# Summing the first heads' queries, keys and values quarter by quarter, in PSUM banks that stay open while the modulation arrives

## The chip, the cores and the metric

One core of one Trainium2 chip runs the whole program. The metric is the device time in microseconds of one execution, the median of several runs; lower is better.

## What is computed

Two transformer blocks and then two mixer layers over 512 latent tokens and 256 context tokens of 1024 features, batch 1. Only the front of the first block matters here:

```
mod_lat = silu(c)    @ ada_w[0] + ada_b[0]       # 6 x 1024: shift, scale, gate, twice
mod_ctx = silu(c_ctx) @ ada_w[0] + ada_b[0]
u_lat = rms_norm(x,   g_mix) * (1 + sc1)  + sh1      # 512 x 1024
u_ctx = rms_norm(ctx, g_mix) * (1 + csc1) + csh1     # 256 x 1024
q, k, v = split(u @ na_wqkv, 3)                      # 16 heads of 64, latent and context
q, k = rms_norm(q, na_q_gain), rms_norm(k, na_k_gain)    # per head
y_lat = neighborhood_attention(q_lat, k_lat, v_lat, k_ctx, v_ctx, rpb) @ na_wo
y_ctx = context_attention(q_ctx, k_ctx, v_ctx) @ na_wo
```

Everything is float32. The kernel writes each matrix operand as a high and a low part (`hi`, `lo`) and sums three products, hi·hi, hi·lo and lo·hi.

## The kernel before

Activations lie feature by feature: `hl` holds the latent tokens as 8 blocks of 128 features by 512 tokens, `hc` the context as 8 blocks by 256. The modulated activations are `uhl`/`ull` (latent, high and low) and `uhc`/`ulc` (context).

**The order of the work.** The kernel is a Python program that issues instructions; a planner orders each engine's instructions before the run, by the program's order and by when it reckons that an instruction's operands are there. It can draw a later instruction ahead of one that isn't ready. At run time each engine takes its own queue strictly in the planned order. Tiles of one name share a fixed number of buffers; a new tile waits until the last reader of the buffer's previous tile is done. `banks(...)` gives names to the eight PSUM banks by turns: `banks(mm="01", ...)` hands out banks 0 and 1 alternately to every projection.

**The start (L595 to L617).** `load_x` issues the activations on SP's DMA queue (3.1 MB). Then a loop over four quarters `b` of the modulation: `ada(0, 0, "AD", b)` loads four pieces of 512 KB of `ada_w` into six borrowed buffers (`vt`, `ky`, `qx`, two each), multiplies them with silu(c) (L183), copies the sums out (L202), turns them into columns (L206) and adds the bias (L216). A quarter gives shift and scale of two feature blocks, and `mod_gain` (L256) the gain. At `b == 1` the token norms `rstd` (L263 to L275) are issued, at `b == 3` the weights of the first head pair's queries and keys (`qk_w(0)`: 4 DMAs of 256 KB, then L128 and L129 split them into `whi`, `wlo`). After the loop stand the modulation of all eight blocks (`modulate`, L278 to L290: product on VectorE, shift on ScalarE, low part on VectorE or GpSimd), the loads of three position biases, `qk_proj(0)` and `v_proj(0)`.

**Projections.** `lin` (L147) sums queries or keys: for each of two column groups j it runs 24 terms (8 feature blocks, three products) into a latent bank (512 columns) and a context bank (256). All high weights come first, the eight low-weight terms last. `tok` (L156) sums the values with the tokens on the partitions: six token tiles of 128, each 24 terms of 256 columns, one PSUM bank each. `v_proj` loads its own weights (2 DMAs of 512 KB). `whi` and `wlo` have two buffers each, the raw weights four.

**Head norms.** `head_norm` (L293 to L308) takes a finished sum from its bank (Square on ScalarE L297, product with the gain on VectorE L298), sums squares over a head by a matmul (L300, into bank 7), and needs three of the six temporaries; `stack_q` and `stack_k` (L327 to L342) then write the high and low parts. One head pair needs four such norms: query latent, query context, key latent, key context.

**The loop behind.** For eight head pairs `hp`, five units `b` each: scores (L347), maximum and exponentials (L314, L650), transposes (L656), attention (L677). At `b == 1` the projections of the next pair are issued (`qk_proj(hp + 1)`, then three tiles of the next values); here `mm` is banks 0 and 1, scores take 3 and 4, transposes 5, attention 6, and low weight parts are made on GpSimd.

Of the kernel before, what the change touches and what calls it, by code (L numbers as in the profile page):

```python
# [19 lines left out]
D = 1024  # L20
# [42 lines left out]
def kernel(ctx: ExitStack, tc: tile.TileContext, A, out, stop_after=None):  # L63
# [83 lines left out]
    def lin(outs, w, ms, k0=0, k1=KD, start=True, stop=True):  # L147

        hi, lo = w
        terms = [(a, i, j) for i in range(k0, k1) for a, j in ((hi, 1), (hi, 2))] + [(lo, i, 1) for i in range(k0, k1)]  # L150
        for n_, (a, i, j) in enumerate(terms):
            for o in outs:
                nc.tensor.matmul(out=o[0], lhsT=a[:, i, ms], rhs=o[j][:, i, :],  # L153
                                 start=(start and n_ == 0), stop=(stop and n_ == len(terms) - 1))

    def tok(ps, wv, xs):  # L156

        hi, lo = wv
        terms = [(x, hi, i) for i in range(KD) for x in xs] + [(xs[0], lo, i) for i in range(KD)]
        for n_, (x, w, i) in enumerate(terms):  # L160
            nc.tensor.matmul(out=ps, lhsT=x[:, i, :], rhs=w[:, i, :], start=(n_ == 0), stop=(n_ == len(terms) - 1))  # L161
# [222 lines left out]
    with tc.tile_pool(name="first", bufs=1) as fp, scratch("scr1", 6, 2):  # L384
# [149 lines left out]
        def neighborhood():  # L534
# [4 lines left out]
            with tc.tile_pool(name="na", bufs=1) as ap_:  # L539
# [4 lines left out]

                def qk_proj(hp, w):
                    qk = []
                    for j in range(2):
                        pl, pc = mm_tile(), mm_tile()[:, :NCTX]
                        lin([(pl, *ul), (pc, *uc)], w, slice(128 * j, 128 * j + 128))
                        g = vec("na_k") if j else nag  # L550
                        if j:
                            y = ky_tile()
                            stack_k(y, LAT, head_norm(pl, NLAT, g))
                            stack_k(y, slice(NLAT, NT), head_norm(pc, NCTX, g))
                            qk.append(y)
                        else:
                            x = qx_tile()
                            lo = next(lows)
                            stack_q((x, lo), LAT, head_norm(pl, NLAT, g))
                            nc.scalar.activation(out=x[:, :, NLAT:QC], in_=x[:, :, 0:64].bitcast(F32), func=AF.Copy)  # L560
                            nc.vector.tensor_copy(out=lo[:, :, NLAT:QC], in_=lo[:, :, 0:64].bitcast(F32))
                            stack_q((x, lo), slice(QC, QC + NCTX), head_norm(pc, NCTX, g))
                            qk.append((x, lo))
                    qks[hp] = qk

                def qk_w(hp, lo_eng=None):
                    return load_w([(0, 128, wqkv[:, 128 * hp:128 * hp + 128]),
                                   (128, 128, wqkv[:, D + 128 * hp:D + 128 * hp + 128])], KD, 256, lo_eng)

                def v_proj(g, ts=range(6)):  # L570
# [898 lines left out]
```

## Time and profile before

| | us |
|---|---|
| median of 3 runs | 2670.5 |
| lowest, highest | 2670.2, 2676.28 |
| the profiled execution, its own time | 2669.24 |
| its span, first to last instruction | 2667.5 |
| TensorE (PE) busy | 2581.6 |
| VectorE (DVE) busy | 1611.9 |
| ScalarE (ACT) busy | 1249.7 |
| GpSimd (POOL) busy | 314.9 |

A row of the timeline gives the start in us, the busy time in us, the engine, the line, the operation, the tile written and the tiles read, the shape and the count; in brackets stands how long the engine idled before it and what ended that. PE's busy time contains modelled ends of pipelined matmuls; from start to start two matmuls can be closer than one lasts. SPq is SP's queue of DMA issues.

### The profile page before, as it was taken

The numbers are of one execution on the slowest core, as the hardware profiler recorded it, in microseconds if no ns is written. First come the engines' busy times: TensorE is split into PE (matmuls) and PEld (weight loads), VectorE is DVE, ScalarE is ACT, GpSimd is POOL, SyncE is SP. The second block draws the span as 40 slices with busy tenths as digits, with TensorE's granted clock in tenths as the row PEclk, the third lists the DMA queues.
The fourth block names the chain that finished last, engine by engine and source line by source line (L and its number), as shares of the span: only waits on it lengthen the run. The fifth ranks groups of instructions, "written<-read, shape, count | busy, mean of one in ns | idle before, by whom it ended". The sixth has DMA issues, their size and how long they took to land.

```text
span 2667.5 us, 40938 instructions
## 1 busy us (share of the span) xinstructions
PE 2581.6 (97%) x15876; PEld 2185.8 (82%) x15876; DVE 1611.9 (60%) x3496; ACT 1249.7 (47%) x2661; POOL 314.9 (12%) x344
## 2 busy tenths in 40 slices
PE   7999999999999999999999999999999999999998
PEld 4877777888888888877788888987778888998887
DVE  5667658676666577688664444755664556523245
ACT  5656556422222223688552323456664554554342
POOL 2221310100000000332010000111101111101011
PEclk9999999999999999999999999999999999999999
DMA  8111324143333342210123333322222232323321
GB/s 258 56 56 53 115 64 156 56 150 113 115 114 118 95 127 64 76 33 17 48 80 98 101 100 95 86 74 67 61 76 79 80 86 80 93 88 95 97 91 54
DMA packets 217634, 237.93 MB, mean 89 GB/s; under 512 B 9824, under 2 KB 179296, under 8 KB 217440
## 3 DMA queue, kind: packets, MB, share of 16 engines
q1 hardware_dynamic: 210464, 229.15, 28.3%
q10 hardware_dynamic: 6976, 6.17, 0.8%
q8 instruction: 125, 2.05, 0.3%
q14 instruction: 69, 0.57, 0.1%
HBM read 233.18 MB, written 2.10 MB: 88 GB/s over the span
## 4 chain that ended last, share of the span: by engine, by line
PE 80%; DVE 10%; ACT 7%; issue 2%; DMA 1%; POOL 0%; DVEq 0%; POOLq 0%; ACTq 0%; SPq 0%
PE mm L153 59%; PE mm L161 7%; PE ST L677 1%; DVE t L281 1%; PE PT L656 1%; PE ST L836 1%; PE PT L819 1%; PE NS L300 1%; DVE acc L269 1%; PE S L347 1%; PE PO L1052 1%; ACT qx L327 1%; DVE wlo L129 1%; ACT whi L128 1%; ACT qx L333 1%
## 5 line engine op out<-in xcount | busy, mean ns | idle before, releaser
L129 DVE TENSOR_TENSOR wlo<-wraw,whi 128x512 fp32r<-128x512 f32 (+1 forms) x580 | 385.7, 704 | 383.6 <-ACT whi L128 248.3
L128 ACT ACTIVATE whi<-wraw 128x512 fp32r<-128x512 f32 (+1 forms) x632 | 353.9, 619 | 475.9 <-PE mm L153 275.1
L153 PE MATMUL mm<-uhl,whi 128*128 128x512 f32 (+1 forms) x1480 | 568.8, 388 | 1.7 <-ACT whi L128 1.6
L153 PE MATMUL mm<-ull,whi 128*128 128x512 f32 (+1 forms) x1480 | 565.6, 385 | 2.9 <-POOL ull L129 2.9
L153 PE MATMUL mm<-uhl,wlo 128*128 128x512 f32 (+1 forms) x1480 | 406.4, 384 | 1.9 <-DVE wlo L129 1.9
L153 PEld LDWEIGHTS mm<-uhl,whi 128*128 128x128 f32 x1480 | 278.0, 188 | 60.4 <-ACT whi L128 4.9
L153 PEld LDWEIGHTS mm<-ull,whi 128*128 128x128 f32 x1480 | 278.2, 188 | 55.2 <-POOL ull L129 4.7
L153 PEld LDWEIGHTS mm<-uhl,wlo 128*128 128x128 f32 x1480 | 268.6, 188 | 55.6 <-DVE wlo L129 2.5
L419 DVE SCALAR_TENSOR_TENSOR hl<-mm,mod,hl 128x512 f32<-128x512 f32 (+1 forms) x156 | 105.3, 680 | 187.5 <-PE mm L153 187.1
L153 PE MATMUL mm<-h1l,whi 128*128 128x512 f32 (+1 forms) x576 | 209.3, 371 | 0.0
L153 PE MATMUL mm<-h1h,whi 128*128 128x512 f32 (+1 forms) x576 | 208.9, 370 | 0.0
L129 POOL TENSOR_TENSOR ull<-t,uhl 128x256 fp32r<-128x256 f32 (+1 forms) x40 | 37.7, 947 | 1091.5 <-ACT uhl L128 997.8
L153 PE MATMUL mm<-h1h,wlo 128*128 128x512 f32 (+1 forms) x576 | 161.8, 369 | 0.0
L161 PE MATMUL mm<-whi,uhl 128*128 128x256 f32 x608 | 152.6, 286 | 0.6 <-DVE t L298 0.5
L161 PE MATMUL mm<-whi,ull 128*128 128x256 f32 x608 | 152.9, 287 | 0.0
L232 DVE SCALAR_TENSOR_TENSOR aacc<-araw,csil,aacc 128x512 f32<-128x512 f32 x196 | 135.2, 746 | 0.0
L475 ACT ACTIVATE t<-mm 128x512 f32<-128x512 f32 (+1 forms) x100 | 47.7, 507 | 171.2 <-PE mm L153 171.2
L153 PE MATMUL mm<-ulc,whi 128*128 128x256 f32 x448 | 124.6, 286 | 1.8 <-POOL ulc L129 1.8
L153 PEld LDWEIGHTS mm<-h1h,whi 128*128 128x128 f32 x576 | 108.6, 189 | 20.1 <-issue 1.0
L153 PE MATMUL mm<-uhc,whi 128*128 128x256 f32 x448 | 124.7, 287 | 0.2 <-ACT uhc L128 0.2
L153 PEld LDWEIGHTS mm<-h1l,whi 128*128 128x128 f32 x576 | 108.6, 189 | 18.7
L161 PEld LDWEIGHTS mm<-whi,uhl 128*128 128x128 f32 x608 | 116.2, 191 | 2.7 <-DVE t L298 1.4
(382 smaller groups left out, 5289.0 us busy)
## 6 DMA issues: line engine op xcount, KB each, us to landing
wraw<-mlp_w SPq DMA_DIRECT2D x128, 512.0 KB, 4.1
wraw<-l_w_in SPq DMA_DIRECT2D x88, 512.0 KB, 4.0
araw<-ada_w SPq DMA_DIRECT2D x112, 256.0 KB, 2.9
wraw<-l_w_out SPq DMA_DIRECT2D x32, 512.0 KB, 3.5
wraw<-ada_w SPq DMA_DIRECT2D x24, 512.0 KB, 4.3
wraw<-l_w_in SPq DMA_DIRECT2D x48, 256.0 KB, 3.4
wraw<-na_wqkv SPq DMA_DIRECT2D x32, 256.0 KB, 4.0
wraw<-swa_wqkv SPq DMA_DIRECT2D x12, 512.0 KB, 3.6
```

Of the source, the lines that this page charges most:

```text
L128: nc.scalar.activation(out=hi, in_=src, func=AF.Copy)
L129: lo_eng.tensor_tensor(out=lo, in0=src, in1=hi.bitcast(F32), op=ALU.subtract)
L153: nc.tensor.matmul(out=o[0], lhsT=a[:, i, ms], rhs=o[j][:, i, :], start=(start and n_ == 0), stop=(stop and n_ == len(terms) - 1))
L161: nc.tensor.matmul(out=ps, lhsT=x[:, i, :], rhs=w[:, i, :], start=(n_ == 0), stop=(n_ == len(terms) - 1))
L232: nc.vector.scalar_tensor_tensor(out=acc[v], in0=raw, scalar=x, in1=acc[v], op0=ALU.mult, op1=ALU.add)
L269: nc.vector.tensor_tensor(out=acc, in0=acc, in1=sq, op=ALU.add)
L281: nc.vector.scalar_tensor_tensor(out=t, in0=h, scalar=gain, in1=r, op0=ALU.mult, op1=ALU.mult)
L300: nc.tensor.matmul(out=st, lhsT=blk, rhs=sq)
L327: nc.scalar.activation(out=x[a, e, c], in_=t[a], func=AF.Copy)
L333: nc.scalar.activation(out=x[b, e, c], in_=t[a], func=AF.Copy)
L419: nc.vector.scalar_tensor_tensor(out=o, in0=ps, scalar=mod[i][:, 8 * which + m, v:v + 1], in1=h, op0=ALU.mult, op1=ALU.add)
L475: nc.scalar.activation(out=a, in_=p, func=AF.Relu)
```

## The change

The four quarters now carry the first projections with them.

- The weights of the first queries and keys are loaded and split right after the activations, ahead of all of `ada_w`; those of the first values right after the first quarter's `ada_w`, their low parts on VectorE.
- Six banks stay open through the loop: banks 0 and 1 for the latent queries and keys, bank 2 for both contexts side by side, banks 3 to 5 for the values, two token tiles in each. A bank that holds two sums is first filled with zeros by a matmul (four in all), as two sums can't both open it.
- After each quarter's `mod_gain` its two feature blocks are modulated, and `lin` and `tok` add the terms of these two blocks (`k0`, `k1`) to the open sums: 12 of the 48 `lin` terms and 36 of the 144 `tok` terms. Only the last quarter closes the banks.
- Behind the loop the head norms stand as before (moved into `qk_heads`); the values leave their banks by three ScalarE copies of 512 columns in place of six of 256.

```diff
-                banks(mm="01234", NS="7", AD="56")
+                w0 = qk_w(0)
+                banks(QL="01", QC="2", V="345", AD="6", NS="7")
+                pq = [bank("QL") for _ in range(2)]
+                pc = bank("QC")
+                pv = [bank("V") for _ in range(3)]
+
+                for x in (pc, *pv):
+                    nc.tensor.matmul(out=x, lhsT=ones, rhs=zero.to_broadcast([128, 512]), start=True, stop=False)
...
                 for b in range(4):
-                    if b == 1:
-                        r = [rstd(h, n) for h, n in ((hlat, NLAT), (hctx, NCTX))]
-                    if b == 3:
-                        w0 = qk_w(0, nc.vector)
                     for _ in ada(0, 0, "AD", b):
                         pass
                     mod_gain(0, "mix", 2 * b, 2 * b + 2)
+                    if b == 0:
+                        r = [rstd(h, n) for h, n in ((hlat, NLAT), (hctx, NCTX))]
+                        wvs[0] = v_w(0)
+                    for k in range(2 * b, 2 * b + 2):
+                        for v, h, u in ((0, hlat, ul), (1, hctx, uc)):
+                            modulate(k, h(k), r[v], gains["gmix0"][:, v, k:k + 1], mod[0][:, k, v:v + 1], u[0][:, k, :], u[1][:, k, :])
+                    for j in range(2):
+                        lin([(pq[j], *ul), (pc[:, 256 * j:256 * j + 256], *uc)], w0, slice(128 * j, 128 * j + 128), 2 * b, 2 * b + 2,
+                            (b == 0, False), (b == 3, b == 3 and j == 1))
+                    for t in range(6):
+                        x, o = (ul, 128 * t) if t < 4 else (uc, 128 * (t - 4))
+                        tok(pv[t // 2][:, 256 * (t % 2):256 * (t % 2) + 256], wvs[0], parts(x, slice(o, o + 128)), 2 * b, 2 * b + 2, False,
+                            b == 3 and t % 2 == 1)
                 scr.pop("ada", None)
-                for k in range(KD):
-                    for v, h, u in ((0, hlat, ul), (1, hctx, uc)):
-                        modulate(k, h(k), r[v], gains["gmix0"][:, v, k:k + 1], mod[0][:, k, v:v + 1], u[0][:, k, :], u[1][:, k, :])
                 for h in range(3):
                     load_bias(h)
-                qk_proj(0, w0)
-                v_proj(0)
+                qks[0] = [qk_heads(j, pq[j], pc[:, 256 * j:256 * j + 256]) for j in range(2)]
+                vts[0] = vt_tile()
+                for x in range(3):
+                    nc.scalar.activation(out=vts[0][:, 2 * x:2 * x + 2, :].rearrange("p t f -> p (t f)"), in_=pv[x], func=AF.Copy)
```

## Rows read from the trace of the kernel before

**Rows 1.** The page, part 1: busy us of each engine, share of the span, instructions

```profile
PE 2581.6 (97%) x15876; PEld 2185.8 (82%) x15876; DVE 1611.9 (60%) x3496; ACT 1249.7 (47%) x2661; POOL 314.9 (12%) x344
```

**Rows 2.** Windows: stretch, length, busy PE, PEld, DVE, ACT, POOL, granted clock, DMA share, GB/s

```profile
0.00:14.79 14.79, 0.00 (x1) 0.00 (x1) 6.67 (x21) 9.12 (x19) 3.79 (x10) 1.00 0.90 292
14.79:20.86 6.07, 6.07 (x28) 2.13 (x29) 2.83 (x7) 2.05 (x4) 0.00 (x0) 1.00 1.09 348
20.86:34.25 13.39, 9.81 (x86) 4.78 (x85) 9.39 (x26) 8.25 (x16) 3.91 (x4) 1.00 1.11 331
34.25:59.68 25.43, 24.79 (x135) 17.23 (x136) 14.96 (x30) 14.01 (x28) 5.06 (x5) 1.00 0.75 229
59.68:81.48 21.80, 19.38 (x152) 18.39 (x150) 14.73 (x23) 14.15 (x32) 9.71 (x8) 1.00 0.17 49
81.48:93.53 12.05, 11.80 (x82) 9.90 (x81) 4.91 (x14) 3.31 (x8) 5.47 (x4) 1.00 0.29 88
93.53:141.06 47.53, 46.11 (x346) 38.72 (x344) 32.13 (x88) 28.68 (x68) 9.74 (x8) 1.00 0.16 45
141.06:189.77 48.71, 45.78 (x344) 38.15 (x343) 33.29 (x88) 30.04 (x71) 14.76 (x12) 1.00 0.24 77
```

**Rows 3.** Waits of PE from 14 to 82 us: total, times, longest

```profile
PE NS L300 <- DVE t L306: 2.4, 2, 2.0
```

**Rows 4.** Timeline: first modulated block, first projection matmul, last quarter's modulation

```profile
24.35 0.72 ACT L289 ACTIVATE uhl<-t,mod 128x512 fp32r<-128x512 f32 x1 [2.46 <-DVE t L281]
...
34.25 0.50 PE L153 MATMUL mm<-uhl,whi 128*128 128x512 f32 x1 [0.24 <-ACT whi L128]
...
46.55 0.24 DVE L216 TENSOR_TENSOR mod<-AD,vecs 128x4 f32<-128x4 f32 x2 [0.81 <-PE AD L206]
```

**Rows 5.** Timeline of SP's queue: the first head pair's weights

```profile
25.36 4.90 SPq L140 DMA_DIRECT2D wraw<-na_wqkv  x4
```

**Rows 6.** Timeline of PE: terms of a later projection, and value terms

```profile
78.60 0.28 PE L161 MATMUL mm<-whi,uhc 128*128 128x256 f32 x1
78.72 0.28 PE L161 MATMUL mm<-whi,ulc 128*128 128x256 f32 x1
...
82.89 0.40 PE L153 MATMUL mm<-ull,whi 128*128 128x512 f32 x1
...
83.25 0.39 PE L153 MATMUL mm<-uhl,whi 128*128 128x512 f32 x1
```

**Rows 7.** Timeline of PE: token norm and two loads of `ada_w`

```profile
14.79 2.07 PE L271 MATMUL NS<-acc,ones 128*128 128x512 f32 x2 [14.79 <-DVE acc L269]
16.79 1.92 PE L183 MATMUL AD<-vt,csil 128*32 128x256 f32 x8
...
25.78 1.06 PE L183 MATMUL AD<-ky,csil 128*32 128x256 f32 x8 [0.83 <-DMA ky<-ada_w]
```

**Rows 8.** Timeline: the chain of the first pair's head norms

```profile
55.52 0.60 ACT L297 ACTIVATE t<-mm 128x512 f32<-128x512 f32 x1 [2.40 <-PE mm L153]
...
56.17 1.12 PE L300 MATMUL NS<-t,blk 128*128 128x512 f32 x2
...
63.78 0.75 DVE L298 TENSOR_SCALAR t<-mm,vecs 128x512 f32<-128x512 f32 x1
...
81.48 0.28 PE L347 MATMUL S<-ky,qx 128*128 128x256 f32 x1
```

**Rows 9.** Timeline: the second pair's weights, first unit, last projection term

```profile
56.04 1.67 ACT L128 ACTIVATE whi<-wraw 128x512 fp32r<-128x512 f32 x3
...
84.86 0.61 PE L656 MATMUL PT<-ident,p 128*128 128x128 f32 x4
...
88.41 1.09 PE L677 MATMUL ST<-pts,vt 128*64 128x128 f32 x16
...
93.53 0.28 PE L347 MATMUL S<-ky,qx 128*128 128x256 f32 x1
...
104.27 0.28 PE L153 MATMUL mm<-uhc,wlo 128*128 128x256 f32 x1
```

More of the change, by code (lines that the diff above doesn't have):

```diff
@@ L149, in lin, with tok @@
         hi, lo = w
+        start, stop = (x if isinstance(x, tuple) else (x,) * len(outs) for x in (start, stop))
         terms = [(a, i, j) for i in range(k0, k1) for a, j in ((hi, 1), (hi, 2))] + [(lo, i, 1) for i in range(k0, k1)]
         for n_, (a, i, j) in enumerate(terms):
-            for o in outs:
+            for o, first, last in zip(outs, start, stop):
                 nc.tensor.matmul(out=o[0], lhsT=a[:, i, ms], rhs=o[j][:, i, :],
-                                 start=(start and n_ == 0), stop=(stop and n_ == len(terms) - 1))
-    def tok(ps, wv, xs):
+                                 start=(first and n_ == 0), stop=(last and n_ == len(terms) - 1))
+    def tok(ps, wv, xs, k0=0, k1=KD, start=True, stop=True):
         hi, lo = wv
-        terms = [(x, hi, i) for i in range(KD) for x in xs] + [(xs[0], lo, i) for i in range(KD)]
+        ks = range(k0, k1)
+        terms = [(x, hi, i) for i in ks for x in xs] + [(xs[0], lo, i) for i in ks]
         for n_, (x, w, i) in enumerate(terms):
-            nc.tensor.matmul(out=ps, lhsT=x[:, i, :], rhs=w[:, i, :], start=(n_ == 0), stop=(n_ == len(terms) - 1))
+            nc.tensor.matmul(out=ps, lhsT=x[:, i, :], rhs=w[:, i, :],
+                             start=(start and n_ == 0), stop=(stop and n_ == len(terms) - 1))
     csil = cst.tile([128, KD, 32], F32, name="csil")
@@ L543, in neighborhood, with qk_heads @@
                 lows = low_tiles(ap_, NT + 64)
+                def qk_heads(j, pl, pc):
+                    g = vec("na_k") if j else nag
+                    if j:
+                        y = ky_tile()
+                        stack_k(y, LAT, head_norm(pl, NLAT, g))
+                        stack_k(y, slice(NLAT, NT), head_norm(pc, NCTX, g))
+                        return y
+                    x = qx_tile()
+                    lo = next(lows)
+                    stack_q((x, lo), LAT, head_norm(pl, NLAT, g))
+                    nc.scalar.activation(out=x[:, :, NLAT:QC], in_=x[:, :, 0:64].bitcast(F32), func=AF.Copy)
+                    nc.vector.tensor_copy(out=lo[:, :, NLAT:QC], in_=lo[:, :, 0:64].bitcast(F32))
+                    stack_q((x, lo), slice(QC, QC + NCTX), head_norm(pc, NCTX, g))
+                    return x, lo
                 def qk_proj(hp, w):
```

25 lines of the change are left out of this document (7 added, 18 removed).

## The prediction

> **What bounds the kernel now.** I began with the page's first part: TensorE (PE) is busy for 97% of the span [rows 1]. A change at the start can therefore gain only what PE idles there; whatever it merely moves from one PE stretch to another is worth nothing. The stretches with their busy times give that idle time [rows 2]: 14.79 us before the first matmul, 13.39 - 9.81 = 3.58 us from 20.86 to 34.25 (the modulation's matrix `ada_w` arrives), 25.43 - 24.79 = 0.64 us up to 59.68, and 21.80 - 19.38 = 2.42 us up to 81.48, where the first scores begin: 21.4 us in all, 6.6 of them after the first matmul. The last two columns of the same rows say what holds the start: the DMA engines are full (share 0.90 to 1.11, 292 to 348 GB/s) until PE takes over. The list of PE's waits names the 2.42 us [rows 3]: matmuls of the head norms that stood in PE's queue until VectorE let go of their bank.
>
> So from 34.25 on PE is full although the projections wait for modulation. The reason is in the kernel's text: before the change, too, the planner let PE begin a projection's terms as each feature block was modulated; the first such matmul stands at 34.25 [rows 4], in the midst of the last quarter's `ada_w`. What the change can add is the values' terms and a start nearer to the first modulated block, which was ready at 25.07 [rows 4].
>
> **The DMAs that move.** Weights of 4 x 256 KB (queries, keys) move from ahead of the last `ada_w` quarter to ahead of the first; 2 x 512 KB (values) move from behind all `ada_w` to behind the first quarter. Each is 1.05 MB, at 348 GB/s [rows 2] 3.0 us of a full queue. On SP's queue the first `ada_w` loads come 3.0 us later, quarters two and three 6.0 us, and the last 3.0 us (it already had one of the two ahead [rows 5]). In the kernel before the last quarter's results were ready at 46.55 [rows 4], but PE got to its last load late, behind projection matmuls; 3 us later in the queue costs there about 0 to 2 us. The biases and the next weights move behind by the same 1.05 MB at most; nobody needs them before 70, so that costs nothing.
>
> **PE's work, counted.** A projection term of 512+256 columns takes 83.25 - 82.89 = 0.36 us, a value term 78.72 - 78.60 = 0.12 us [rows 6]. A quarter of the features is 12 of the first (4.3 us) and 36 of the second (4.3 us): 8.6 us, four of them 34.3 us. That is the same count as before; the change removes no matmul. An `ada_w` load is 8 matmuls in 1.06 us [rows 7], a quarter's transposes 0.6 us. The four added zero matmuls have no row of their own; the nearest is the one of the same shape and type, two records in 2.07 us at 14.79 [rows 7]. Four of them are 8.3 us, from about 2 us on, when their operands are set: they end near 10.5, inside the 14.79 us of idle, and cost nothing; with the cover gone they would cost 8.3 us. Splits of the two weights are moved, not added (16 instructions on ScalarE and VectorE); those of the values' weights, some 2.5 us on each, now fall beside the first modulation and may delay it by up to 1.5 us. Three wide copies of the values in place of six narrow ones are even.
>
> **When PE ends this stage.** The first modulated block comes 1.5 to 3.0 us after 25.07; I take 27.5, as the queue is full then. From there PE has 34.3 + 12 loads x 1.06 + 3 x 0.6 = 48.8 us, so the values end at 76.3 if it never waits. It may: the planner gives PE, among what is ready, what the program names first. I read that from 82 to 95: PE ran one pair's projection to its end (93.53) before the scores of the next unit, which the program names later, and VectorE had 4.91 us of work in those 12.05 us [rows 2, 9]. In the changed text each quarter's projections stand ahead of the next quarter's `ada_w` matmuls. So PE, once behind, finishes a quarter's 8.6 us before it does the small transposes of the next, and the next modulation (about 2 us to its first block, 5 to its second) starts late. Waits of 0 (the matmuls of a later quarter fill them) to 4 us; I take 2: values done at 78.
>
> **What comes late then: the head norms.** Before, the first query sum was complete at 55.5, and the chain Square, norm, stacking ran from there to the scores at 81.48 [rows 8]: 26.0 us, all of it under PE work, the values' 17 us above all. After, the query sum closes only with the last quarter, some 4.3 us ahead of the values' end: at 73.7. Nothing in the diff shortens the chain, so scores begin near 73.7 + 26.0 = 99.7, 18 us later than before. Two edits of the chain's neighbours, the values' copies and the order of the two context halves in one bank, are below 1 us.
>
> What covers the 21.7 us from 78 to 99.7 is the point that decides. There are the norms' own four matmuls (two of 1.12 us [rows 8], two of half the columns, some 3.5 us) and the next pair's projections, which before ended at 104.3 [rows 9]. Their first half (24 terms, 8.6 us) needs a weight buffer (free at about 75, when the first pair's last term is done, then split by ScalarE) and banks 0 and 1, free once the chain has read queries and keys. Keys were read 8.3 us after the chain's start, at 63.78 [rows 8]; after: 82. So the first half is done by about 90. The second half needs the same two banks again, hence its readers, hence temporaries: six, three for each head norm, freed as the first four norms end. The third norm began 8.3 us into the chain, so its temporaries and the fourth's go free in the last third of the 26 us; I estimate 19 to 21 us after its start, 93 to 95. PE idles 3 to 5 us; then 8.6 us bring it to about 102, where PE before was at 104.3. Before, however, had done by then both heads' scores, transposes (0.61 us each) and attention (1.09 us) of the first unit and half the scores of the second: 13 score matmuls of 0.12 us and 2.3 us, 3.9 us [rows 9]. So PE stands at 102 + 3.9 - 104.3 = 1.6 us later. VectorE's later start on the units costs a little more, 0 to 4 us, as it is far from full afterwards (32.13 of 47.53 us [rows 2]); I take 1.4. **Sum: +3 us.** What is behind is kept to the end, as PE has hardly a wait in which to make it up: the profiled execution is 2669.24 us, of which 2667.5 is span; plus 3 is 2672.2. It lies 1.3 us under the median of the three runs, so against the median I say 2673.5.
>
> **A rule against it.** The granted clock reads 1.00 in every stretch [rows 2], the upper level of 2.4 GHz; still the first `ada_w` load's eight matmuls took 1.92 us and a later one's 1.06, one right after a wait of 0.83 us too [rows 7]. After the change PE waits longer between its first loads. The Trainium skill, "TensorE: Matmul & The Clock Gate", section "HAM oscillation — how this bites in real kernels", says that short bursts between DMA waits throw the array back to its low clock again and again. By that, the first quarter would run at the slow pace; the row after the wait speaks against it.
>
> **Rivals.**
> - *The chain is bare (slower).* If the next pair's first half doesn't get into the hole (its weights wait for the buffer, or bank 1 for the keys' reading), PE loses those 8.6 us as well: +3 + 8.6, 2682; with nothing but norms under the chain 99.7 - 81.48 = +18, 2689. It decides at 78 us: is there a matmul of the second pair before the scores of the first? For it: one rotation of two banks and six temporaries. Against: weights of the second pair were split from 56 on in the kernel before, as soon as the buffer was free [rows 9]. Price 2684, chance 0.22.
> - *Slow pace in the first quarter.* By the pace of 1.92 against 1.06 us [rows 7], nearly twice the time for up to 13 us of work, partly hidden by waiting: +5 to +13, 2680. Chance 0.04.
> - *Ahead for good (faster).* The next projections leave the stretch in which VectorE had little to do, and the head pairs behind it, which have 1.4 and 2.9 us of PE wait in some 48 us (47.53 - 46.11 in the first of them [rows 2]), close up: 7 pairs x 2 us = -14, 2657. Against: only one pair's first half can be ahead at a time. Chance 0.09.
> - *It doesn't do what it says.* The planner may still put the values last, as PE is full anyway; then head norms start early as before, and only the DMA shift counts: 0 to +2, 2671.5. Chance 0.05, inside "no change".
>
> **How the numbers follow.** The forecast itself has 0.60; its own range is 2666 to 2679 (best: no waits after 27.5, -3.5 us with the 1.7 us of waits between 81.48 and 141.06 gone as well, and the first block 1 us earlier; worst: 4 us of quarter waits and 4 on VectorE). A measurement of this kernel tells about 0.3%, 8 us, from no change. Faster by more: 0.09 + 0.01 of the forecast = 0.10. Slower by more: 0.22 + 0.03 of the pace, 0.01 of the forecast = 0.26. Within: 0.64. The range leaves out one in ten on each side: 2661 to 2686, which takes in the half-bare chain and half of the closing up.
>
> **What the changed profile would show.** First projection matmul at 27 to 28 instead of 34.25; the first Square of the head norms at 72 to 76 instead of 55.5; first scores at 96 to 102; second pair's projections beginning before the first scores; PE wait of 3 to 5 us around 90. I am wrong if the norms start before 65 (then the gain is real), or if the hole before the scores is over 10 us.

## The result, and the profile after

The changed kernel takes 2687.55 us (median of six, 2685.9 to 2690.09) against 2672.11 (2670.2 to 2676.28) of the kernel before on the same chip: **ratio 1.0056, 95% interval 1.0046 to 1.0066**, some 15 us slower. The prediction was 2673.5 with a range of 2661 to 2686; the time lies above the range. The sign of the sum was right, its size was not. The profiled execution of after is 2685.9 us, its span 2684.1. All lines of the code lie a few lines later in it: the Square that was L297 is L300, `lin` is L154, `tok` L163, the modulation's matmuls L186, its transposes L209.

The page, part 1, of after; against [rows 1] TensorE's share is the same and its busy time 13 us higher, on the same work and 8 more instructions (the four zero matmuls, 6 us of it from 1.92 to 7.91):

```profile
PE 2594.5 (97%) x15884; PEld 2193.5 (82%) x15884; DVE 1611.7 (60%) x3496; ACT 1250.0 (47%) x2658; POOL 311.0 (12%) x344
```

Windows of after, the stretches and columns of [rows 2], the two from 81.48 to 141.06 in one:

```profile
14.79:20.86 6.07, 4.34 (x11) 1.51 (x12) 5.24 (x12) 3.99 (x8) 0.00 (x0) 0.50 1.11 339
20.86:34.25 13.39, 10.79 (x52) 5.94 (x53) 6.53 (x15) 6.15 (x12) 0.96 (x1) 0.64 1.04 330
34.25:59.68 25.43, 23.02 (x174) 18.19 (x172) 4.94 (x16) 3.34 (x6) 2.96 (x4) 1.00 0.78 237
59.68:81.48 21.80, 18.09 (x122) 14.18 (x120) 7.63 (x18) 7.34 (x13) 3.93 (x4) 1.00 0.01 3
81.48:141.06 59.58, 51.13 (x334) 41.95 (x333) 40.74 (x94) 42.94 (x91) 23.83 (x20) 0.97 0.25 73
```

Two things differ from before. TensorE idles 8.45 us from 81.48 to 141.06 where it idled 1.67, 2.41 up to 59.68 where it idled 0.64, and 3.71 in the next stretch instead of 2.42. And its granted clock reads 0.50 from 14.79, the lower level of 1.2 GHz, and 0.64 in the next stretch, a mixture of both levels, where before reads 1.00. In the first of these two stretches the reading of before isn't its pace: its first load of `ada_w` took 1.92 us there [rows 7], just as the one of after at 17.99 did. The rows differ in the second: before's loads take 1.06 us from 20.86 on, while after's projection terms from 27.74 to 34 run at about half pace. DMA is all but silent (0.01) from 59.68 to 81.48, so nothing waits for a transfer there.

Timeline of VectorE, the four steps that turn a quarter's matmuls into modulation (before: 23.09, 28.01, 34.05 and 46.55, the last in [rows 4]):

```profile
25.71 0.23 DVE L219 TENSOR_TENSOR mod<-AD,vecs 128x4 f32<-128x4 f32 x2 [0.70 <-PE AD L209]
44.36 0.23 DVE L219 TENSOR_TENSOR mod<-AD,vecs 128x4 f32<-128x4 f32 x2 [0.70 <-PE AD L209]
59.23 0.23 DVE L219 TENSOR_TENSOR mod<-AD,vecs 128x4 f32<-128x4 f32 x2 [0.70 <-PE AD L209]
74.18 0.23 DVE L219 TENSOR_TENSOR mod<-AD,vecs 128x4 f32<-128x4 f32 x2 [0.70 <-PE AD L209]
```

They come 15 to 19 us apart. Timeline of PE between the first and the third quarter shows why; the waiting time stands in the brackets:

```profile
27.74 0.80 PE L154 MATMUL QL<-uhl,whi 128*128 128x512 f32 x1 [2.07 <-ACT uhl L292]
...
35.28 0.73 PE L154 MATMUL QL<-uhl,whi 128*128 128x512 f32 x2
...
41.80 0.40 PE L163 MATMUL V<-wlo,uhc 128*128 128x256 f32 x2
42.13 1.06 PE L186 MATMUL AD<-ky,csil 128*32 128x256 f32 x8
43.72 0.61 PE L209 MATMUL AD<-sel,adar 128*128 128x4 f32 x4 [0.53 <-DVE adar L205]
...
46.51 0.50 PE L154 MATMUL QL<-uhl,whi 128*128 128x512 f32 x1
...
55.80 0.40 PE L163 MATMUL V<-wlo,uhc 128*128 128x256 f32 x2
...
57.03 1.03 PE L186 MATMUL AD<-qx,csil 128*32 128x256 f32 x8
58.59 0.61 PE L209 MATMUL AD<-sel,adar 128*128 128x4 f32 x4 [0.53 <-DVE adar L205]
```

PE does the first quarter's terms to the end (41.80) and only then the last load of the second quarter and its transposes (43.72). It then has little to do until the next block is modulated (46.51), does that quarter to its end (55.80), and again turns to the modulation last (58.59). The modulation's matmuls don't wait for their data; they stand behind. The list of PE's waits from 27.7 to 86 us:

```profile
PE QL L154 <- ACT uhl L292: 4.1, 2, 2.1
PE QL L154 <- POOL ull L129: 1.7, 3, 0.6
PE AD L209 <- DVE adar L205: 1.6, 3, 0.5
PE AD L186 <- PE AD L209: 0.7, 2, 0.4
```

All four are waits of the modulation for itself. The last is for its bank: the change leaves one bank (6) to the modulation's sums, which had two (5 and 6). e24 below has one bank as well and takes the time of the kernel before, so this isn't what costs. Timelines of ACT and PE, the head norms' chain (before: Square 55.52, norm 56.17, scores 81.48 [rows 8]):

```profile
80.53 0.60 ACT L300 ACTIVATE t<-QL 128x512 f32<-128x512 f32 x1 [1.57 <-PE QL L154]
...
85.51 0.40 PE L163 MATMUL V<-wlo,uhc 128*128 128x256 f32 x2
85.75 1.02 PE L303 MATMUL NS<-t,blk 128*128 128x512 f32 x2
...
95.25 0.56 PE L154 MATMUL mm<-uhc,whi 128*128 128x256 f32 x1 [2.39 <-DVE t L301]
...
102.52 1.07 PE L186 MATMUL AD<-wraw,csil 128*32 128x256 f32 x16 [1.78 <-DVE t L301]
...
106.44 0.50 PE L154 MATMUL mm<-uhl,whi 128*128 128x512 f32 x1 [1.84 <-DVE t L301]
...
107.25 0.36 PE L350 MATMUL S<-ky,qx 128*128 128x256 f32 x1
```

The values end at 85.75; the chain from Square to scores takes 26.7 us, and matmuls of the second pair run inside it. The scores start 25.8 us later than before. Of that, 16 us are left at the eighth head pair's query scaling (406.36 against 389.98), and the profiled times differ by 16.7.

### The profile page after: what moved, and what is told of

It reads as the page before. It is cut to its first block, busy times and chain, and to the rows that moved or that the text cites. A ratio compares the mean times of both kernels' runs of the same rounds, so it can differ in the third digit from the quotient of the medians.

```text
span 2684.1 us, 40954 instructions
## 1 busy us (share of the span) xinstructions
PE 2594.5 (97%) x15884; PEld 2193.5 (82%) x15884; DVE 1611.7 (60%) x3496; ACT 1250.0 (47%) x2658; POOL 311.0 (12%) x344
## 4 chain that ended last, share of the span: by engine, by line
PE 81%; DVE 10%; ACT 7%; issue 2%; POOL 0%; DMA 0%; DVEq 0%; POOLq 0%; ACTq 0%; SPq 0%
PE mm L154 59%; PE mm L163 7%; PE ST L701 1%; DVE t L284 1%; PE PT L680 1%; DVE acc L272 1%; PE ST L860 1%; PE PT L843 1%; PE NS L303 1%; PE S L350 1%; ACT qx L336 1%; PE AD L186 1%; ACT qx L330 1%; PE PO L1076 1%; PE S L351 1%
## 5 line engine op out<-in xcount | busy, mean ns | idle before, releaser
L154 PE MATMUL mm<-uhl,whi 128*128 128x512 f32 (+1 forms) x1464 | 563.2, 388 | 3.2 <-DVE t L301 1.8
L154 PE MATMUL mm<-ull,whi 128*128 128x512 f32 (+1 forms) x1464 | 559.5, 385 | 2.5 <-POOL ull L129 2.5
L154 PE MATMUL mm<-uhl,wlo 128*128 128x512 f32 (+1 forms) x1464 | 400.5, 384 | 1.8 <-DVE wlo L129 1.8
L154 PEld LDWEIGHTS mm<-uhl,whi 128*128 128x128 f32 x1464 | 275.0, 188 | 61.2 <-DVE t L301 5.7
L154 PEld LDWEIGHTS mm<-ull,whi 128*128 128x128 f32 x1464 | 275.3, 188 | 53.9 <-POOL ull L129 3.7
L154 PEld LDWEIGHTS mm<-uhl,wlo 128*128 128x128 f32 x1464 | 265.5, 188 | 54.5 <-DVE wlo L129 2.4
L154 PE MATMUL mm<-h1l,whi 128*128 128x512 f32 (+1 forms) x576 | 209.3, 371 | 0.0
L154 PE MATMUL mm<-h1h,whi 128*128 128x512 f32 (+1 forms) x576 | 208.9, 370 | 0.0
L129 POOL TENSOR_TENSOR ull<-t,uhl 128x256 fp32r<-128x256 f32 (+1 forms) x40 | 37.7, 947 | 1119.1 <-ACT uhl L128 1025.4
L154 PE MATMUL mm<-h1h,wlo 128*128 128x512 f32 (+1 forms) x576 | 161.8, 369 | 0.0
L163 PE MATMUL mm<-whi,uhl 128*128 128x256 f32 x576 | 143.7, 284 | 1.7 <-DVE t L301 1.2
L163 PE MATMUL mm<-whi,ull 128*128 128x256 f32 x576 | 145.0, 287 | 0.0
L478 ACT ACTIVATE t<-mm 128x512 f32<-128x512 f32 (+1 forms) x100 | 47.7, 507 | 171.5 <-PE mm L154 171.5
L154 PEld LDWEIGHTS mm<-h1h,whi 128*128 128x128 f32 x576 | 108.6, 189 | 20.0 <-issue 1.0
L154 PEld LDWEIGHTS mm<-h1l,whi 128*128 128x128 f32 x576 | 108.6, 189 | 18.7
L154 PE MATMUL mm<-uhc,whi 128*128 128x256 f32 x432 | 120.8, 288 | 2.4 <-DVE t L301 2.4
L154 PE MATMUL mm<-ulc,whi 128*128 128x256 f32 x432 | 120.3, 286 | 1.6 <-POOL ulc L129 1.6
L154 PEld LDWEIGHTS mm<-h1h,wlo 128*128 128x128 f32 x576 | 101.8, 189 | 19.3
```

The lines of the kernel that those rows point to most:

```text
L129: lo_eng.tensor_tensor(out=lo, in0=src, in1=hi.bitcast(F32), op=ALU.subtract)
L478: nc.scalar.activation(out=a, in_=p, func=AF.Relu)
```

## The experiments

Each ratio is against the kernel before on the same chip, from 4 to 11 executions of the variant and 7 to 27 of the kernel before; square brackets give its 95% interval. Differences between two variants are uncertain by some 2 to 4 us. A table of all stands at the end of this section.

**Parts of the change undone.** e1_values_behind sums the values whole, behind the head norms:

```diff
-                    for t in range(6):      # in the loop over quarters b
-                        tok(..., 2 * b, 2 * b + 2, False, b == 3 and t % 2 == 1)
+                for t in range(6):          # after qks[0] = [qk_heads(...)]
+                    tok(..., 0, KD, False, t % 2 == 1)
```

> The changed kernel, but the values are summed whole behind the head norms in program order (their weights are loaded as in the change, their banks stay open). My theory: the change loses because (a) a quarter's 8.6 us of projections stand ahead of the next quarter's modulation matmuls on PE, and (b) all sums close together, so the head norms have no PE work over them. With the values behind, each quarter holds only 4.3 us and the 17 us of values cover the norms again: first Square near 62, first scores 83 to 88, time 2674 (2671 to 2678). Rival 1, the earlier weights (6 us more of DMA ahead of the modulation) are what costs: stays at 2682 or above. Rival 2, PE's slow pace in the first 34 us: 2682 or above as well.

1.0030 [1.0018, 1.0041]; modulations at 40.1, 50.3 and 60.4, Square at 66.7. The 2679.9 us lie between the theory (2674) and the rivals (2682). Of the 15 us half is gone, where almost all was expected to go: about 7 us go with the values' terms, 8 with something else.

e2_modulation_first puts the modulation of quarter b+1 ahead of the terms of quarter b (in short):

```diff
-                for b in range(4):
-                    ada(b); mod_gain(b); modulate(b)
-                    terms(b)
+                for b1 in range(5):
+                    if b1 < 4:
+                        ada(b1); mod_gain(b1); modulate(b1)
+                    if b1 > 0:
+                        terms(b1 - 1)
```

> The changed kernel, but each quarter's ada_w matmuls, gain and modulation stand in the program ahead of the projections of the quarter before; nothing else moves. Theory: only part (a) of the loss is undone: values end at 79 to 81 instead of 86, first scores near 101 instead of 107, time 2681 (2678 to 2684), the bare head norms remain. If the bare head norms are all of the loss: 2686 to 2689. If the order on PE is all of it: 2672 to 2676.

1.0020 [1.0011, 1.0029], 2676.9 us: the order of the program text alone is worth 10 us, more than the 6.5 expected. The stage now runs somewhat ahead of the forecast of the changed kernel (values end at 75.48, first Square at 69.02, first scores at 96.87 us; forecast 78, 73.7, 99.7), and the time is 5 us above before, where 3 were forecast. Its windows show PE without a gap where after had 2.41 and 3.71 us:

```profile
34.25:59.68 25.43, 25.43 (x213) 20.24 (x202) 9.21 (x28) 6.68 (x12) 4.78 (x6) 1.00 0.77 233
59.68:81.48 21.80, 21.80 (x139) 19.31 (x138) 6.38 (x10) 12.38 (x23) 12.17 (x11) 1.00 0.24 70
81.48:141.06 59.58, 52.82 (x371) 44.06 (x370) 46.80 (x119) 40.62 (x93) 13.89 (x12) 0.94 0.18 55
```

e4_heads_first moves the head norms ahead of the last quarter's value terms:

```diff
+                    if b == 3:
+                        qks[0] = [qk_heads(j, pq[j], pc[:, 256 * j:256 * j + 256]) for j in range(2)]
                     for t in range(6):
```

> The changed kernel, but the head norms stand in the program ahead of the last quarter's values, as their first matmul waited from 81.5 to 85.75 us behind the values on PE. Theory: norms' first matmul 4 us earlier, first scores near 103 to 104, time 2684 (2682 to 2686). If PE's count of work alone decides: no change, 2687.

1.0056 [1.0041, 1.0071], first Square at 80.62, scores at 105.5: no gain in the time beyond the noise, where 3.5 us were expected. The chain's place in the text is not what costs most.

**The moved loads alone.** e3_dma_only is the kernel before with nothing but the two loads in their new places; e7_qk_weights_early moves only the first of them.

```diff
                 load_x(eng=nc.sync)
+                w0 = qk_w(0)
 ...
                         r = [rstd(h, n) for h, n in ((hlat, NLAT), (hctx, NCTX))]
-                    if b == 3:
-                        w0 = qk_w(0, nc.vector)
+                        wvs[0] = load_w([(0, 256, wqkv[:, 2 * D:2 * D + 256])], KD, 256)   # e3 only
```

> The kernel before with only the loads moved as the change moves them: query and key weights ahead of all ada_w, value weights behind the first quarter. Theory: 0 to +3 us, 2672 to 2675, since the last quarter comes 3 us later in the queue and PE has other work. Rival 1 (the loads are the cause): 2680 or more.

> The kernel before with only the query and key weights moved ahead of all ada_w (1.05 MB); the value weights stay behind. It splits the cost of the moved loads (13 us) by load. If the cost comes from ada_w arriving later in pieces with PE gaps between them: one load does half of it, 2676 to 2680. If it needs projection terms in the midst of the ada_w matmuls, which both loads allow: 2680 to 2685. If bytes alone count (3 us of queue, nothing else): 2671 to 2674.

e3: 1.0055 [1.0040, 1.0070], e7: 1.0045 [1.0028, 1.0062]. This was the surprise of the study: moving 2.1 MB, which was to cost 0 to 2 us, costs nearly as much as the whole change. e3's timeline of PE, from the first quarter's transposes to the second's:

```profile
25.66 0.68 PE L206 MATMUL AD<-sel,adar 128*128 128x4 f32 x4 [0.53 <-DVE adar L202]
28.41 0.73 PE L153 MATMUL mm<-uhl,whi 128*128 128x512 f32 x2 [2.07 <-ACT uhl L289]
...
31.28 1.92 PE L183 MATMUL AD<-ky,csil 128*32 128x256 f32 x8
...
39.45 0.61 PE L206 MATMUL AD<-sel,adar 128*128 128x4 f32 x4 [0.21 <-DVE adar L202]
```

With the weights in hand early, the planner sets projection terms between the modulation's matmuls. The matmuls on the second quarter's first `ada_w` load come up only at 31.28, behind a wait for the first modulated block; in the kernel before they ran from 22.98, as no projection could start ahead of 34.25 [rows 4]. The load itself must have landed some 4 us earlier: in e16, described next, it is issued 0.6 us later than in e3, no projection term stands ahead, and the same matmuls wait for the load alone and start at 27.38:

```profile
27.38 1.37 PE L183 MATMUL AD<-ky,csil 128*32 128x256 f32 x8 [1.17 <-DMA ky<-ada_w]
```

**Is it the bytes, the order, or the buffers?** e16_order_kept is e3 with one more condition, that no projection term is issued ahead of the third quarter's transposes, which gives PE the order of the kernel before. e17_more_buffers is e3 with ten buffers for `ada_w` instead of six.

```diff
+                    if b == 2:
+                        turned = scr["turned"]        # the transposes' instruction
 ...
-                qk_proj(0, w0)
-                v_proj(0)
+                with tc.issue_after(turned.ins):
+                    qk_proj(0, w0)
+                    v_proj(0)
```

> The kernel before with both loads moved to their new places (as in e3_dma_only), and TensorE held to the order of the kernel before: no projection term may stand ahead of the transposes of the third quarter's modulation. Theory (the cost of the moved loads is the order: with the weights in hand early, projection terms are set between the modulation's own matmuls, which then free the six borrowed buffers late and so issue the modulation's loads late): the modulation's times are about 26, 31, 37 and 48 us (28.0, 34.1 and 46.6 before for the last three), the first Square of a head norm at 56 to 59 us instead of 67.8, and the time is 1.000 to 1.002 of the kernel before. Rival (the bytes themselves, 2.1 MB ahead of the modulation's loads, cost it): last modulation still at 58 to 59, Square at 67, ratio 1.0045 to 1.0055.

> The kernel before with both loads moved (as in e3_dma_only), and the modulation's weights are loaded into ten rotating buffers instead of six (the four of raw weights join the six borrowed ones). TensorE's interleaved order stays. If the buffers are the link by which the order delays the loads: the loads run ahead, the last of the modulation's loads has landed by about 45 us, the last modulation falls to 50 to 54 us, Square to 60 to 63, ratio 1.001 to 1.003. If TensorE's order alone is the delay (its matmuls of the modulation stand behind terms that must be done first): modulation at 57 to 59, ratio 1.0045 to 1.0055 as without the buffers. If the bytes: the same 1.0045 to 1.0055, with the loads landing no earlier.

e16: 1.0022 [1.0013, 1.0032]; e17: 1.0048 [1.0033, 1.0063]. So **the order costs about 9 us** (e3 against e16), and hardly by way of the buffers: e17 issues its last `ada_w` load at 35.67, e3 at 43.81, and e17's last modulation still falls at 57.06. What is left in e16, 6 us, lies at the upper end of what I expected. Its last modulation, and the one of e23_one_load_order_kept, where only the first load is moved and the order kept likewise:

```profile
50.61 0.23 DVE L216 TENSOR_TENSOR mod<-AD,vecs 128x4 f32<-128x4 f32 x2 [0.81 <-PE AD L206]
```

```profile
47.43 0.24 DVE L216 TENSOR_TENSOR mod<-AD,vecs 128x4 f32<-128x4 f32 x2 [0.80 <-PE AD L206]
```

> The kernel before with only the query and key weights moved to the front (as in e7_qk_weights_early, 1.0045) and TensorE held to the order of the kernel before, as in e16_order_kept (1.0022). The same bytes now lie ahead of the last modulation as in the kernel before, where these weights came ahead of the last quarter. Theory (two costs: the order, some 9 us, and the 1.05 MB of the value weights, which are new ahead of the last modulation, some 4 to 6 us): last modulation back at 46 to 48 us (46.6 before, 50.6 in e16), ratio 0.9995 to 1.0010. Rival (all that is left in e16 is the gate on the projections or the early weights themselves, not the value load's bytes): last modulation at 49 to 51, ratio 1.0015 to 1.0025.

e23: 1.0009 [1.0000, 1.0018]. Against e7, its like without the order kept, it gives the order's price a second time, 0.0036 or 10 us. Between e23 and e16 lies the values' load, 1.05 MB more ahead of the last modulation: 3.2 us there (3.0 by the queue's rate) and 0.0013, or 3.5 us with some 2 us of uncertainty, in the time. **The bytes cost about what they take**; e26 against e24 below shows it again.

**Half pace.** e5_warm (after, 16 more zero matmuls), e9_first_and_warm (the same in e2) and e14_dma_only_warm (e3 with 20) raise the granted clock; in each, eight stand between 14.8 and 29 us. e27_dma_only_start_warm and e28_start_warm have twelve at the very start in all and none later.

```diff
-                for x in (pc, *pv):
-                    nc.tensor.matmul(out=x, lhsT=ones, rhs=zero.to_broadcast([128, 512]), start=True, stop=False)
+                for i, x in enumerate((pc, *pv) * 3):
+                    nc.tensor.matmul(out=x, lhsT=ones, rhs=zero.to_broadcast([128, 512]), start=i < 4, stop=False)
 ...
                         wvs[0] = v_w(0)
+                        for x in (pc, *pv) * 2:                       # e5, e9
+                            nc.tensor.matmul(out=x, lhsT=ones, ..., start=False, stop=False)
```

> The changed kernel with 16 more zero matmuls on the open banks (8 ahead of everything, 8 behind the first quarter's modulation), which add nothing but keep PE busy from 2 us to the first projections. Theory now: besides the order on PE, the change spends 27.7 to 34 us at the granted clock of 0.50 (1.2 GHz), which before it left at 20.5, as PE had been busy without a gap; it costs 3 to 6 us, partly by late buffers for ada_w. So granted clock 1.00 from about 8 us on and 2682 to 2684 against 2687.5. Rival (order on PE and bare head norms are all): 2686 to 2689.

> The kernel before with only the loads moved (2684.7) plus 20 zero matmuls into an unused bank, so that PE doesn't fall to 0.50 between the later loads of ada_w. Theory: the moved loads themselves cost 0 to 3 us; the other 10 came from PE at half pace among the ada_w matmuls, which freed the six ada_w buffers late and starved the queue (DMA share 0.37 at 36 to 38 us). So 2674 to 2677. Rival (6 us more of DMA ahead of the modulation is the cost): stays at 2683 to 2686.

> The kernel before with both loads moved (as in e3_dma_only, 1.0055) and twelve matmuls with zeros at the very start, which end by about 14.5 us in time that TensorE idles; unlike e14_dma_only_warm none stands later, so none can delay a matmul of the modulation. Theory (the half pace of the first loads' matmuls lies in time that would be waiting anyway): granted clock higher from 14.8 to 34 us, yet first Square at 66.5 to 68, ratio 1.0045 to 1.0065. Rival (in e14 the gain of the pace was eaten by its eight later matmuls; TensorE is busy 43.3 us up to the Square against 36.5 in the kernel before with the same work, so the half pace costs some 4 to 7 us): Square at 61 to 64.5, ratio 1.0025 to 1.004.

> The changed kernel with its four zero matmuls done three times over at the start (twelve, ending by about 14.5 us), and none later, unlike e5_warm. Theory (half pace hidden): modulations within 1 us of 25.7, 44.4, 59.2, 74.2, Square at 79.5 to 80.7, ratio 1.005 to 1.006. Rival (half pace costs the 3 us that TensorE's work from 27.7 to 34.3 loses at a granted 0.53, and more before): second modulation at 40 to 42, Square at 76 to 78, ratio 1.0035 to 1.0045.

> Next quarter's modulation ahead of the projections (as in the run before this one, 2676.9) and the 16 zero matmuls together. Theory: the two causes are apart, so their gains add: 2671 to 2674. If the slow pace is hidden by waiting for ada_w: 2676 to 2678.

e5 1.0067 [1.0052, 1.0082], e14 1.0056 [1.0041, 1.0071], e27 1.0043 [1.0027, 1.0060], e28 1.0059 [1.0044, 1.0074], e9 1.0030 [1.0018, 1.0042] against e2's 1.0020: no gain outside the intervals. Windows of e14 and of e27, from 20.86:

```profile
20.86:34.25 13.39, 12.10 (x66) 5.30 (x62) 6.50 (x15) 5.74 (x11) 0.00 (x0) 1.00 1.09 343
```

```profile
20.86:34.25 13.39, 10.79 (x52) 5.23 (x54) 6.49 (x15) 6.04 (x12) 0.04 (x1) 0.54 1.06 335
```

e14 has the full clock, and its last modulation is 1.1 us earlier than e3's. But its later zero matmuls themselves take some 8 us of PE. e27 avoids these and loses the clock again:

```profile
18.28 1.06 PE L183 MATMUL AD<-vt,csil 128*32 128x256 f32 x8 [2.37 <-DMA vt<-ada_w]
...
23.21 1.92 PE L183 MATMUL AD<-vt,csil 128*32 128x256 f32 x8
```

So the price of the half pace by itself was not settled. Up to 26 us it was small: in e24 (below) the clock reads 0.50 and 0.83 in these two stretches and the load at 23.44 takes 1.92 us, yet its ratio is 1.0005. What after adds to this is the half pace from 27.7 to 34. In e5 the first modulation comes 2.2 us later than in after and the second 0.4 later: with the full clock 1.8 us of that delay were made up, out of 15.

**Two more of the same kind.** e18_first_more_buffers (e2 with ten buffers) and e21_first_values_behind_buffers (e1 and e2 together, with ten buffers):

> The changed kernel with the next quarter's modulation ahead of a quarter's projection terms (as in e2_modulation_first, 1.002), and ten buffers for the modulation's loads instead of six. Theory (buffers held late): modulations some 3 to 6 us earlier than 38.7, 47.2, 59.1, Square at 64 to 66 instead of 69.0, ratio 1.0000 to 1.0010. Rival (TensorE itself is full from 34 us on, so an earlier load frees nothing): Square within 1 us of 69.0 and ratio 1.0015 to 1.0025.

> The changed kernel with three edits together: the next quarter's modulation ahead of a quarter's terms, the values summed whole behind the head norms (as in e1_values_behind, 1.003), and ten buffers for the modulation's loads. What is left of the change is queries and keys by quarters. Theory (what costs time is whatever TensorE does ahead of the modulation's matmuls, and each edit takes a part of it away): last modulation at 50 to 54 us, Square at 57 to 61, values behind it as in the kernel before, ratio 0.999 to 1.001. Rival (open banks or the half-pace first quarter carry a cost of their own): Square later than 63 and ratio over 1.002.

e18 1.0018 [1.0008, 1.0027], e21 1.0032 [1.0019, 1.0045]. Buffers give nothing here either, and e1's and e2's gains don't add up: in e21 the planner still puts terms among the modulation's matmuls (last modulation 57.9). Its Square, 64.3, and its ratio are those of the rival, a cost of the open banks or of the half pace; the next two runs test that.

**Is summing by quarters itself at fault?** e24_queries_keys_by_quarters keeps queries and keys by quarters, with each quarter's terms held behind the next quarter's transposes, the values' load behind all `ada_w`, and the values whole behind the norms. e26_queries_keys_value_load_early is e24 with the values' load where the change has it.

```diff
+                    with tc.issue_after(scr["turned"].ins):      # transposes of quarter b + 1
                         for j in range(2):
                             lin([(pq[j], *ul), ...
 ...
-                        if b == 0:
+                        if b1 == 3:                                   # e24; e26: b1 == 0
                             wvs[0] = v_w(0)
```

> The changed kernel, of which only the queries and keys by quarters are left: the value weights are loaded behind the last quarter's modulation weights and the values summed whole behind the head norms, and the terms of a quarter may not stand ahead of the transposes of the next quarter. Theory (the costs are the order and the value load's bytes, and both are gone): modulations at 26, 32, 39 and 46 us, first Square at 51 to 55 (55.5 before), ratio 0.998 to 1.0005. Rival (summing by quarters in open banks has a cost of its own, or the half-pace stretch has): Square later than 58, ratio over 1.001.

> As e24_queries_keys_by_quarters, but the value weights are loaded where the changed kernel loads them, ahead of the second quarter's modulation weights. Theory: the bytes put each later modulation 3 to 6 us back and with them the end, ratio 1.0012 to 1.0022 above that of e24. Rival (the load is hidden, as the prediction had it at 0 to 2 us): ratio within 0.0007 of e24.

e24: 1.0005 [0.9997, 1.0014], e26: 1.0020 [1.0011, 1.0029]. The Square of e24, 57.5, is 2.5 us later than expected but ahead of the rival's 58. Open banks and quarter sums cost nothing that can be told; they also gain nothing. e24's first scores are at 80.16, 1.3 us ahead of before, and the gain is gone by the second pair (query scaling at 95.67 against 94.25). The early load puts 4 us on it.

**All together**, sorted by the last modulation (us into the profiled run):

| run | modulations | first Square | ratio |
|---|---|---|---|
| *queries, keys and values whole* | | | |
| before | 23.1 28.0 34.1 46.6 | 55.5 | 1 |
| e23 first load early, order kept | 26.1 30.9 37.7 47.4 | 56.1 | 1.0009 |
| e16 both loads early, order kept | 26.3 34.0 40.9 50.6 | 59.3 | 1.0022 |
| e17 both early, ten buffers | 25.3 38.1 47.6 57.1 | 66.5 | 1.0048 |
| e14 both early, zeros | 27.5 39.0 48.5 58.0 | 67.2 | 1.0056 |
| e7 first load early | 26.7 37.8 47.2 58.3 | 67.2 | 1.0045 |
| e27 both early, zeros at start | 26.7 39.4 48.8 58.3 | 67.5 | 1.0043 |
| e3 both loads early | 26.4 40.1 49.6 59.1 | 67.8 | 1.0055 |
| *queries and keys by quarters* | | | |
| e24 held, value load late | 26.5 31.3 39.5 47.7 | 57.5 | 1.0005 |
| e26 held, value load early | 25.3 37.4 45.6 53.8 | 60.7 | 1.0020 |
| e21 modulation first | 25.7 38.9 48.4 57.9 | 64.3 | 1.0032 |
| e1 as the change has it | 25.3 40.1 50.3 60.4 | 66.7 | 1.0030 |
| *values by quarters too* | | | |
| e2 modulation first | 25.5 38.7 47.2 59.1 | 69.0 | 1.0020 |
| e9 e2 with zeros | 27.6 39.3 48.0 59.8 | 69.8 | 1.0030 |
| e18 e2, ten buffers | 26.6 40.6 49.1 60.9 | 70.9 | 1.0018 |
| after | 25.7 44.4 59.2 74.2 | 80.5 | 1.0056 |
| e4 head norms first | 25.7 44.4 59.3 74.3 | 80.6 | 1.0056 |
| e28 zeros at start | 26.6 44.4 59.3 74.3 | 81.3 | 1.0059 |
| e5 zeros | 27.9 44.8 59.7 74.6 | 81.3 | 1.0067 |

In every run the first Square follows the last modulation by 6 to 10 us, however many terms were summed ahead. In the first group a later last modulation is paid in full: 12.5 us from before to e3 cost 0.0055, 14.7 us. In the second, 12.7 us from e24 to e1 cost 0.0025, 6.7 us. So early sums seem to give back a part of the delay that making them early causes, by this pair about half; with the intervals of the two ratios it may be a quarter or three quarters.

## Why the prediction was wrong, point by point

**The loads: the first failed step.** I costed them at 0 to 2 us, on the argument that PE reached the last `ada_w` load late anyway. Two things were wrong. The bytes are paid: 3.5 us for the 1.05 MB of the values (e16 against e23). And I took the modulation's place among the other matmuls of the kernel before for given, while it hung on the late landing of the first projection weights. When these came early, the planner used them, and that cost 9 us (e3 against e16; 10 by e7 against e23). In the change the same weight of order shows as after against e2: 1.0056 against 1.0020, 10 us.

**Zero matmuls**: hidden, as said; 1.9 to 7.9 us, inside the idle time. Those of after didn't keep the clock up.

**First projection matmul at 27.5**: 27.74.

**Values done at 78: the second failed step**, though its mechanism was the one foreseen (a quarter's projections ahead of the next quarter's matmuls). From 27.74 to 85.75 are 58.0 us for the 48.8 us of work that I counted, 9.2 too many. Windows of after:

```profile
27.74:34.25 6.51, 6.51 (x22) 4.06 (x24) 4.11 (x8) 3.33 (x7) 0.96 (x1) 0.53 0.98 311
34.25:85.75 51.50, 45.38 (x328) 36.55 (x325) 13.07 (x34) 14.00 (x26) 10.31 (x11) 1.00 0.39 118
```

6.51 us at a granted 0.53 did the work of 3.5, 3.0 lost; 51.50 - 45.38 = 6.1 us idle, where I took 2 and set 4 as the end. "The matmuls of a later quarter fill them" holds for the next quarter's loads alone (two of them between 43.72 and 46.51); its terms need its modulation, which stands behind. Three rounds of it at about 2 us each was there to be multiplied out. That this order is the cause, e2 shows: with the next modulation first the values end at 75.48.

**The chain**: 26.0 us predicted, 26.7 measured; it starts with the last quarter's sum, as said, but at 80.5 instead of 73.7, and scores at 107.25 instead of 99.7. Both are late by what the values' end is late.

**The hole before the scores**: the second pair's first half did get into it, but it ended at about 100 us instead of 90, and the second half began at 106.44 instead of 93 to 95. PE's waits there are 2.39, 1.78 and 1.84 us, 6.0 in all, against 3 to 5; the stretch from 85.75 on holds 21.50 us with 15.18 busy. The rows show the key's reading by VectorE, the stretch, and two parts of it:

```profile
94.44 0.75 DVE L301 TENSOR_SCALAR t<-QL,vecs 128x512 f32<-128x512 f32 x1
...
85.75:107.25 21.50, 15.18 (x77) 11.04 (x76) 12.40 (x20) 15.32 (x32) 10.05 (x9) 0.92 0.47 137
...
95.00:97.00 2.00, 1.75 (x8) 1.75 (x9) 1.46 (x3) 1.92 (x4) 0.00 (x0) 0.58 0.72 233
97.00:99.00 2.00, 2.00 (x12) 2.00 (x12) 1.18 (x5) 0.89 (x3) 0.73 (x1) 0.57 0.02 8
```

"Keys were read 8.3 us after the chain's start" was too short: it was 13.9 us (94.44 against 80.53), as the norm's first matmul at 85.75 stood behind the values on PE. That reading frees the bank for which PE waits 2.39 us at 95.25. Behind the wait PE is at the lower clock for a while (0.58 and 0.57): 16 context terms take the 3.5 us from 95.25 to 98.78, where 0.12 us each would be 1.9.

**The sum**: +3 was predicted, +15 measured. The values' end explains 7.75 of the 12 missing (85.75 against 78). The rest lies in the hole: the late reading of the keys and the lower clock behind the wait are rows of it, but what each costs at the end of the run isn't shown; e4, in which the keys are read at 89.84, gains nothing. In the experiments' terms the 15 us add up: 10 for the order (after against e2), 4 for the values' load (e26 against e24; 3.5 by e16 against e23), 1 for all else (e24 against before), each with 2 to 3 us of uncertainty. This is one way to divide them and no proof that the parts are apart: e1 and e2 show that such gains need not add.

**The rivals.** *The chain is bare* gave 2684, near the measured time, but that is luck in the main: it was to decide by whether the second pair gets into the hole, and it did. Only its wait for "bank 1 for the keys' reading" came true, with the 2.39 us. *Slow pace* is real in the rows, as the granted 0.50 and 0.64 show, and I was wrong to let one row of the kernel before (1.06 us after a wait of 0.83) speak against it: e27's load at 18.28 also still took 1.06 after a wait of 2.37, and the one at 23.21 1.92. The Trainium skill, "TensorE: Matmul & The Clock Gate", section "HAM oscillation — how this bites in real kernels", says that short bursts between waits for DMA keep throwing the array back to the low clock; the trace agrees as to the clock (granted 0.54 in e27, 0.50 and 0.64 in after), though here the first load behind the wait still ran at full pace. As to the time, 1.8 us were given back at the second modulation when the clock was raised, and none at the end, so its +5 to +13 us are not shown. *Ahead for good*: nothing is ahead; e24, which comes nearest, loses its 1.3 us within one pair. *It doesn't do what it says*: it does.

## What to carry to other kernels

A load is not only bytes: in a kernel whose order a planner makes, a late load also keeps its consumers out of the way of others, and moving it early lets them in ahead of the work that everything else waits for. Before giving an engine more to do "while it waits", ask what stands behind the new work in its queue: in a pipeline of producer and consumer on one engine, the next producer step goes first (e2), and what one round waits is multiplied by the rounds. Work that is pulled ahead in a stage where the engine is full gains only the idle time of that stage, here some 7 us by [rows 2], of which e24 could keep none.

## What the runs showed of the hardware

Twelve zero matmuls that kept TensorE busy up to 14.5 us didn't carry its clock through the loads (e27): a wait of 2.37 us, one load of eight matmuls at 1.06 us, a further wait, then the load at 23.21 at 1.92 us, granted 0.54 from 20.86 to 34.25. The eight later ones of e14, set between the loads, held 1.00 through the same stretch. From 14.79 to 20.86 the DMA engines were full in every run (share 1.09 to 1.12, 335 to 348 GB/s), so a load that is put ahead puts the next ones back by its bytes, 3 us for 1.05 MB. Beyond these, how late `ada_w` was used was decided on TensorE, as e17 shows, whose loads were all issued by 37 us and used until 56.
